# Eight of the 22 down-projection rows as four pairs with seven products each, beside classical columns of the other half of the tokens

## The chip, the cores and the metric

The kernel runs on one core of one Trainium2 chip. The metric is the device time of one execution in microseconds (us); the profile's span runs from its first to its last instruction. PE is TensorE, DVE VectorE, ACT ScalarE, POOL GpSimd, SP SyncE (all bulk DMAs are issued from its queue).

## The reference, cut to what matters

One layer of a hybrid decoder for 1024 prompt tokens and 64 sample tokens, 1088 columns in all, with shared weights. After input projection, sparse attention and short convolution comes the part that matters here:

```
def ffn_and_ple(x, p, norm_ffn, w_gate_up, w_down, norm_ple, w_ple, w_ple_gate):
    h = rmsnorm(x, norm_ffn)
    gu = h @ w_gate_up                       # 1024 -> 2 * 2816
    g, u = gu[..., :D_FF], gu[..., D_FF:]
    x = x + (jax.nn.silu(g) * u) @ w_down    # 2816 -> 1024
    gate = jax.nn.sigmoid(rmsnorm(x, norm_ple) @ w_ple_gate)
    return x + (p @ w_ple) * gate
```

All in float32. D_FF = 2816 is 22 blocks of 128, called rows here; D_MODEL = 1024 is 8 blocks, called k.

## The kernel before

**Precision.** Each float32 operand is split into a rounded `hi` part (ScalarE copy to fp32r) and the remainder `lo` (a subtraction on VectorE or GpSimd). A product is three matmuls: hi x hi, hi x lo, lo x hi.

**Layout.** The 1088 tokens lie along the free dimension and are cut into two problems p = 0 and 1 of PW = 544 columns, each of two tiles of CW = 272. The residual stream x1 lies in SBUF for the whole second half. Gate-up results go to DRAM (`m_scr`, one row of 544 columns at a time) and come back for the down projection.

**Gate-up** already uses seven products. `add_pair` loads four weight blocks and forms four sums on VectorE (`wsum`); `prep` copies each of seven combinations to `hi` on ScalarE, and `low` subtracts, on VectorE for kinds 6, 5 and 4, on GpSimd for the others. `factors` builds the seven token combinations of a problem (`fac[p]`, 28 tiles of 272 in a buffer `A` for problem 0, `B` for problem 1). `run_pair` runs 7 x 12 = 84 matmuls a pass; `GateUp.take` adds each product out of PSUM on VectorE (product 1 on ScalarE). The entries of `order` run one pair for problem 0 and then for problem 1; only the pairs 0 and 1 run for problem 0 alone, then pair 2 for both, then 0 and 1 for problem 1.

**Down projection before** (`down_pass`, `run_rows`, `down_rows`, `evac_down`). The 22 rows are four groups, `GR = [(0, 4), (4, 6), (10, 6), (16, 6)]`, which take the buffers A and B in turn. `down_rows` fetches the rows of a group for both problems into small places (`Q`, ten of 544 columns) and `row_in` splits them, every other one on GpSimd. `run_rows` makes, for one k, one PSUM tile per column tile out of all rows of the group; `evac_down` adds it to x1 on VectorE. Groups 0 and 3 use tiles of 272 columns, groups 1 and 2 three tiles of 384, 384 and 320. Groups 0 to 2 run both problems k by k; group 3 runs problem 0 for all k and then problem 1, so that problem 0's norm (`add_square`, `rstd`, `norm_rows`, which writes h3 into A) lies beside problem 1's matmuls. Then the gate pass (`ple_pass`) of each problem follows on h3.

**Order.** All instructions are put in a fixed order by `Weaver`, a planner with a cost for each operation: streams are generators, a main stream issues the matmuls, side streams are taken first when their event, places and planned times allow it. Weights are prepared ahead in eight slots and up to four raw places (`Weights.pump`), five PSUM banks `pj` take the products. The planner's costs know nothing of engines that hinder each other. TensorE's order is written out in `order`.

Of the kernel before, what the change touches and what calls it, by code (L numbers as in the profile page):

```python
# [20 lines left out]
P = 128  # L21
# [295 lines left out]
def hybrid_decoder_step(ctx, tc, I, O):  # L317
# [87 lines left out]
    class Weights:  # L405
# [114 lines left out]
        def prep(self, it, s):  # L520
# [42 lines left out]
            def low():  # L563
                (W.tt if kind in (6, 5, 4) else W.pool_tt)(flat(l), src, flat(h).bitcast(F32), OP.subtract, n)
                it["split"] = True
                self.free(*free)
# [1401 lines left out]
    def norm_rows(p, gfun, ev):  # L1968
# [4 lines left out]
        yield ev_left  # L1973
        if p == 0:
            N_["h3"] = [Rows(apool, f"A_{e}", f"h3_{e}") for e in ("hi", "lo")]
# [101 lines left out]

    ev_ms = [[Ev(), Ev()] for _ in range(NF)]
    GR = [(0, 4), (4, 6), (10, 6), (16, 6)]
# [5 lines left out]
    def down_rows():  # L2085

        for g, (f0, n) in enumerate(GR):
            free = ev_gu[g] if g < 2 else ev_gr[g - 2]
            yield ev_near
            for p in range(2):  # L2090
                left, ahead = [n], []
                for j in range(n):
                    yield ev_ms[f0 + j][p]
                    yield {"Q": 1}
                    q, = getq(1)
                    ahead.append((j, q, W.dma(q, m_scr[f0 + j, :, p * PW:(p + 1) * PW])))
                    if free.t is None and len(ahead) < min(4, n):
                        continue
                    if g not in M:
                        yield free  # L2100
                        r = "AB"[g % 2]
                        M[g] = [Rows(apool if r == "A" else N_["bp"], f"{r}_{e}", f"m{g}_{e}", n) for e in ("hi", "lo")]
                    for j_, q_, t in ahead:
                        W.spawn(row_in(M[g], j_, p, q_, t, left, ev_md[g][p]))
                    ahead.clear()

    def row_in(rows, j, p, q, t, left, ev):
        W.cur.t = max(W.cur.t, t)
        yield None
        s = split_row(rows, j, p, q, j % 2 == 1)  # L2110
        next(s)
        yield None
        next(s, None)
        left[0] -= 1
        if left[0] == 0:
            ev.t = W.cur.t

    def evac_down(g, k, p, h, ps):
        c0, n = DOWN_H[p][h] if p in DOWN_H else (p * PW + h * CW, CW)
        xs = N_["x1"][:, k, c0:c0 + n]  # L2120
        W.tt(xs, ps[:, :n], xs, OP.add, n)
        free_ps()
        if g == len(GR) - 1 and h == 1:
            W.spawn(add_square(p, k, n_down, g_ple, ev_h3, how=norm_rows))

    DOWN_H = {f"c{c}": {c // 2: CH[c]} for c in range(3)}
# [182 lines left out]
    def down_pass(g, ks, ps):  # L2309
        f0, n = GR[g]  # L2310
        bs = [rows_of(I["w_down"], k, lambda *a: evac_down(g, *a), row0=f0 * P, nk=n) for k in ks]
        evs, halves = ev_md[g], None
        if 0 < g < len(GR) - 1:
            ps, halves, evs = tuple(DOWN_H), DOWN_H, dict(zip(DOWN_H, (evs[0], evs[1], evs[1])))
        order.append(("rows", bs, ps, lambda: M[g], evs, 0, ev_gr[g] if ks[-1] == KT - 1 else None, None, halves))
# [13 lines left out]
    for g_ in range(len(GR) - 1):  # L2329
        down_pass(g_, (0, 1), (0, 1))  # L2330
        for k_ in range(2, KT):
            down_pass(g_, (k_,), (0, 1))
    n_before = len(order)
    for p_ in range(2):
        for k_ in range(KT):
            down_pass(len(GR) - 1, (k_,), (p_,))
# [35 lines left out]
    def run_pair(x, p, last, ev_done):  # L2372
        items, sink = x
        yield ev_h2[p]
        blocks = range(4)
        tot = 3 * len(blocks)
        for q_, i in enumerate(ORDER):
# [8 lines left out]
            for kk, b in enumerate(blocks):  # L2386
                th, tl = factor(p, i, b)
# [117 lines left out]
```

## Time and profile before

| | |
|---|---|
| median of 3 runs | 1964.89 us |
| profiled execution | 1964.83 us |
| its span | 1963.1 us |
| TensorE busy | 1911.7 us, 97% |
| VectorE, ScalarE, GpSimd busy | 65%, 36%, 38% |
| granted TensorE clock, mean | 0.992 |
| gate-up: matmuls from 1098.3 to | 1571.4 us |
| down projection | 1571.8 to 1837.0 us |
| gate pass and final norm | 1837.0 to 1963.1 us |

A window's line gives its length and each engine's busy time with its count of instructions in parentheses, in the order PE, PEld (weight loads), DVE, ACT, POOL, then the granted clock, DMA share and GB/s. A timeline line gives start, duration, engine, line, operation, out<-in and count, with idle time before it and its releaser in brackets.

### The profile page before, as it was taken

The page shows a single profiled execution, that of the slowest core. Times are in us where ns is not written, and L with a number is a line of the kernel's source. Part 1 is how long each engine was busy: PE and PEld are TensorE (multiplying, and loading weights), DVE is VectorE, ACT ScalarE, POOL GpSimd, SP SyncE. Part 2 cuts the span into 40 slices and gives each one's busy share as a digit, 9 for nine tenths or more (in the row PEclk, how much of TensorE's full clock was granted, in tenths as well). Part 3 has the DMA queues.
Part 4 walks back from the last instruction along what each step waited for, and adds up shares of the span by engine and source line. Part 5 has one row for each costly group of instructions (what it writes and reads, how often), then busy time and mean ns, then how long its engine had stood idle before and what let it go on. Part 6 is the DMA issues. An engine that isn't in the chain of part 4 may idle for free.

```text
span 1963.1 us, 35813 instructions
## 1 busy us (share of the span) xinstructions
PE 1911.7 (97%) x13337; PEld 1852.5 (94%) x13337; DVE 1278.8 (65%) x2691; ACT 701.7 (36%) x1403; POOL 750.5 (38%) x662
## 2 busy tenths in 40 slices
PE   8999989999999999999999899999999999999998
PEld 5998889998999989989999899999999999999998
DVE  6646999999999975214338885665665643314754
ACT  5355433213443235323334542322322322213543
POOL 2543455223322233114444342322322454424883
PEclk9999999999999999999999999999999999999999
DMA  4565335222322222546443432222222443212343
GB/s 154 170 190 151 99 105 145 54 56 66 85 65 52 63 74 54 154 126 198 126 146 121 145 101 76 77 83 70 79 83 66 139 150 99 89 47 85 105 135 118
DMA packets 293688, 206.27 MB, mean 105 GB/s; under 512 B 28912, under 2 KB 273192, under 8 KB 293514
## 3 DMA queue, kind: packets, MB, share of 16 engines
q1 hardware_dynamic: 293190, 203.63, 35.1%
q8 instruction: 105, 1.72, 0.4%
q14 instruction: 69, 0.57, 0.1%
q10 hardware_dynamic: 324, 0.36, 0.1%
HBM read 152.61 MB, written 51.31 MB: 104 GB/s over the span
## 4 chain that ended last, share of the span: by engine, by line
PE 81%; DVE 9%; issue 3%; DMA 3%; POOL 2%; SPq 1%; ACT 0%; DVEq 0%; POOLq 0%; ACTq 0%
PE pj L155 44%; PE pj L191 26%; PE at L187 4%; PE po L187 3%; PE pt L198 3%; DVE junk L1235 2%; SPq L164 1%; DVE ru L136 1%; POOL wl L151 1%; DVE cum L1271 1%; PE at L198 1%; DMA wraw<-in_w_in 1%; DMA qh<-qh_scr 0%; DVE scores L140 0%; DVE cv L140 0%
## 5 line engine op out<-in xcount | busy, mean ns | idle before, releaser
L151 POOL TENSOR_TENSOR wl<-wraw,wh 128x512 fp32r<-128x512 f32 (+2 forms) x234 | 302.4, 1295 | 660.2 <-ACT wh L132 636.5
L191 PE MATMUL pj<-h_hi,wh 128*128 128x384 f32 (+2 forms) x1197 | 404.9, 338 | 0.6 <-DVE ru L136 0.3
L191 PE MATMUL pj<-h_hi,wl 128*128 128x384 f32 (+2 forms) x1197 | 394.0, 329 | 0.7 <-POOL wl L151 0.7
L191 PE MATMUL pj<-h_lo,wh 128*128 128x384 f32 (+2 forms) x1197 | 393.6, 329 | 0.0
L132 ACT ACTIVATE wh<-wraw 128x512 fp32r<-128x512 f32 (+2 forms) x234 | 142.3, 611 | 295.8 <-PE pj L155 136.7
L191 PEld LDWEIGHTS pj<-h_hi,wh 128*128 128x128 f32 (+1 forms) x1197 | 226.4, 189 | 10.7 <-issue 6.3
L191 PEld LDWEIGHTS pj<-h_lo,wh 128*128 128x128 f32 (+1 forms) x1197 | 226.3, 189 | 2.8
L191 PEld LDWEIGHTS pj<-h_hi,wl 128*128 128x128 f32 (+1 forms) x1197 | 225.7, 189 | 1.8 <-POOL wl L151 1.1
L155 PE MATMUL pj<-f_hi,wl 128*128 128x272 f32 x704 | 204.3, 290 | 5.5 <-DVE wl L136 5.5
L155 PE MATMUL pj<-f_hi,whl 128*128 128x272 f32 x1056 | 206.0, 288 | 0.0
L155 PE MATMUL pj<-f_hi,wh 128*128 128x272 f32 x704 | 204.0, 290 | 0.3 <-DVE q_lo L136 0.2
L155 PE MATMUL pj<-f_lo,wh 128*128 128x272 f32 x704 | 203.3, 289 | 0.2 <-DVE f_lo L136 0.2
L136 DVE TENSOR_TENSOR x<-pj,x 128x272 f32<-128x272 f32 (+2 forms) x144 | 67.0, 469 | 173.4 <-PE pj L155 170.0
L155 PE MATMUL pj<-m_hi,wh 128*128 128x272 f32 (+2 forms) x586 | 176.1, 300 | 1.2 <-DVE x L136 0.7
L155 PE MATMUL pj<-m_hi,wl 128*128 128x272 f32 (+2 forms) x586 | 175.7, 300 | 0.0
L155 PE MATMUL pj<-m_lo,wh 128*128 128x272 f32 (+2 forms) x586 | 175.5, 300 | 0.0
L155 PEld LDWEIGHTS pj<-f_hi,whl 128*128 128x128 f32 x1056 | 168.7, 189 | 0.0
L155 PE MATMUL pj<-f_lo,whl 128*128 128x272 f32 x528 | 152.3, 288 | 0.0
L155 PEld LDWEIGHTS pj<-f_hi,wl 128*128 128x128 f32 x704 | 133.6, 190 | 5.9 <-DVE wl L136 5.9
L155 PEld LDWEIGHTS pj<-f_hi,wh 128*128 128x128 f32 x704 | 133.4, 189 | 0.6 <-issue 0.6
L155 PEld LDWEIGHTS pj<-f_lo,wh 128*128 128x128 f32 x704 | 133.3, 189 | 0.4 <-DVE f_lo L136 0.4
L151 POOL TENSOR_TENSOR whl<-wraw,whl 128x512 fp32r<-128x512 f32 x68 | 94.2, 1388 | 74.0 <-ACT whl L132 72.0
(376 smaller groups left out, 4488.1 us busy)
## 6 DMA issues: line engine op xcount, KB each, us to landing
wraw<-in_w_in SPq DMA_DIRECT2D x112, 256.0 KB
wraw<-in_w_gate_up SPq DMA_DIRECT2D x96, 256.0 KB
wraw<-in_w_down SPq DMA_DIRECT2D x40, 256.0 KB
wraw<-in_w_out SPq DMA_DIRECT2D x32, 256.0 KB
wraw<-in_w_ple_gate SPq DMA_DIRECT2D x32, 256.0 KB
x<-in_x_prompt SPq DMA_DIRECT2D x13, 512.0 KB
m_scr<-q_lo SPq DMA_DIRECT2D x19, 272.0 KB
q_lo<-m_scr SPq DMA_DIRECT2D x18, 272.0 KB
```

The source lines that it names most:

```text
L132: self.nc.scalar.activation(out, in_, func, **kw)
L136: self.nc.vector.tensor_tensor(out, a, b, op=op)
L151: self.nc.gpsimd.tensor_tensor(out, a, b, op=op)
L155: self.nc.tensor.matmul(ps, l, r, start=start, stop=stop)
L164: self.nc.sync.dma_start(out, in_)
L187: self.nc.tensor.matmul(ps, l, r, start=start, stop=stop)
L191: self.nc.tensor.matmul(ps, l, r, start=start, stop=stop)
L198: self.nc.tensor.transpose(ps, in_, ident)
L1235: nc.vector.tensor_scalar(junk[:m, :L], score[q], cand[:m, i:i + 1].bitcast(F32), None, op0=op, op1=OP.add, accum_out=cnt[:m, i:i + 1])
L1271: nc.vector.tensor_tensor_scan(cum, eq, eq, 0.0 if last is None else last, op0=OP.add, op1=OP.bypass)
```

## The change

- `GR` becomes two groups of seven classical rows, 0 to 6 and 15 to 21. Rows 7 to 14 become four pairs of blocks (7+b, 11+b); with the output columns k and k+4 (k = 0 to 3) they form four `DownPair` items a problem, each seven products, run by `run_pair` with `down=True`.
- `pairs_for` fetches the eight rows of a problem and `factors` builds the combinations, for problem 0 in buffer B (after gate-up has left it), for problem 1 in buffer A (after group 0 has left it). Group 1's rows go into B after problem 0's last pair (`ev_sx`).
- The order in each half g is: classical rows of group g for problem 0, all eight k; then, for i = 0 to 3, the pair i of problem g and the classical column k = i of problem 1; then k = 4 to 7 of problem 1. Down weights are therefore loaded and split once for each problem. All column tiles have 272 columns.
- A pair's seven remainders are all subtracted by VectorE (`"dve"`), and all row splits too (`row_in`). `DownPair.finish` adds the two results to x1 with 544 columns each.
- The square of k for the norm waits for pair k's addition (`last_add`); `norm_rows` also waits for the last pair of problem 1 (`ev_sy`), since h3 takes buffer A.

```diff
@@ -561,7 +561,7 @@
             W.act(flat(h), src, AF.Copy, n)
 
             def low():
-                (W.tt if kind in (6, 5, 4) else W.pool_tt)(flat(l), src, flat(h).bitcast(F32), OP.subtract, n)
+                (W.tt if kind in (6, 5, 4) or kind and "dve" in q else W.pool_tt)(flat(l), src, flat(h).bitcast(F32), OP.subtract, n)
                 it["split"] = True
                 self.free(*free)
             if kind == 0:
@@ -1971,6 +1971,7 @@
         ns, ev_r = rs.pop(p)
         yield ev_r
         yield ev_left
+        yield ev_sy
         if p == 0:
             N_["h3"] = [Rows(apool, f"A_{e}", f"h3_{e}") for e in ("hi", "lo")]
         yield {"at": 2, "Q": 1}
@@ -2075,8 +2076,26 @@
                 ev_ms[f][p].t = W.cur.t + 2.5
             W.later(store)
 
+    def last_add(p, k):
+        yield ev_sk[p][k]
+        yield from add_square(p, k, n_down, g_ple, ev_h3, how=norm_rows)
+
+    class DownPair(GateUp):
+
+
+        def finish(self, p, q1, q2):
+            for q, k in ((q1, self.f), (q2, self.f + 4)):
+                yield None
+                xs = N_["x1"][:, k, p * PW:(p + 1) * PW]
+                W.tt(xs, xs, q, OP.add, PW)
+                giveq(q)
+                ev_sk[p][k].t = W.cur.t
+
     ev_ms = [[Ev(), Ev()] for _ in range(NF)]
-    GR = [(0, 4), (4, 6), (10, 6), (16, 6)]
+    GR = [(0, 7), (15, 7)]
+    F_S = 7
+    ev_fd, ev_sx, ev_sy = [Ev(), Ev()], Ev(), Ev()
+    ev_sk = [[Ev() for _ in range(KT)] for _ in range(2)]
     ev_near = Ev()
     ev_gu, ev_gr = [Ev(), Ev()], [Ev() for _ in GR]
     ev_md = [[Ev(), Ev()] for _ in GR]
@@ -2084,30 +2103,58 @@
 
     def down_rows():
 
-        for g, (f0, n) in enumerate(GR):
-            free = ev_gu[g] if g < 2 else ev_gr[g - 2]
-            yield ev_near
-            for p in range(2):
-                left, ahead = [n], []
-                for j in range(n):
-                    yield ev_ms[f0 + j][p]
-                    yield {"Q": 1}
-                    q, = getq(1)
-                    ahead.append((j, q, W.dma(q, m_scr[f0 + j, :, p * PW:(p + 1) * PW])))
-                    if free.t is None and len(ahead) < min(4, n):
-                        continue
-                    if g not in M:
-                        yield free
-                        r = "AB"[g % 2]
-                        M[g] = [Rows(apool if r == "A" else N_["bp"], f"{r}_{e}", f"m{g}_{e}", n) for e in ("hi", "lo")]
-                    for j_, q_, t in ahead:
-                        W.spawn(row_in(M[g], j_, p, q_, t, left, ev_md[g][p]))
-                    ahead.clear()
+        yield ev_near
+        yield from rows_for(0, "A", ev_gu[0])
+        yield from pairs_for(0, "B", ev_gu[1])
+        yield from rows_for(1, "B", ev_sx)
+        yield from pairs_for(1, "A", ev_gr[0])
+
+    def pairs_for(p, r, free):
+        yield free
+        pool = N_["bp"] if r == "B" else apool
+        fac["d", p] = [pool.tile([P, 28, CW], F32, tag=f"{r}_{e}", name=f"fd{p}_{e}") for e in ("hi", "lo")]
+        left = [4]
+
+        def done():
+            left[0] -= 1
+            if left[0] == 0:
+                ev_fd[p].t = W.cur.t
+        for b in range(4):
+            for f in (F_S + b, F_S + 4 + b):
+                yield ev_ms[f][p]
+            yield {"Q": 3}
+            qs, t = getq(3), 0.0
+            for q, f in zip(qs, (F_S + b, F_S + 4 + b)):
+                t = W.dma(q, m_scr[f, :, p * PW:(p + 1) * PW])
+            W.spawn(pair_in(p, b, qs, t, done))
+
+    def pair_in(p, b, qs, t, done):
+        W.cur.t = max(W.cur.t, t)
+        yield None
+        yield from factors(("d", p), b, *qs, Ev(), done)
+
+    def rows_for(g, r, free):
+        f0, n = GR[g]
+        for p in range(2):
+            left, ahead = [n], []
+            for j in range(n):
+                yield ev_ms[f0 + j][p]
+                yield {"Q": 1}
+                q, = getq(1)
+                ahead.append((j, q, W.dma(q, m_scr[f0 + j, :, p * PW:(p + 1) * PW])))
+                if free.t is None and len(ahead) < min(4, n):
+                    continue
+                if g not in M:
+                    yield free
+                    M[g] = [Rows(apool if r == "A" else N_["bp"], f"{r}_{e}", f"m{g}_{e}", n) for e in ("hi", "lo")]
+                for j_, q_, t in ahead:
+                    W.spawn(row_in(M[g], j_, p, q_, t, left, ev_md[g][p]))
+                ahead.clear()
 
     def row_in(rows, j, p, q, t, left, ev):
         W.cur.t = max(W.cur.t, t)
         yield None
-        s = split_row(rows, j, p, q, j % 2 == 1)
+        s = split_row(rows, j, p, q, False)
         next(s)
         yield None
         next(s, None)
@@ -2116,14 +2163,13 @@
             ev.t = W.cur.t
 
     def evac_down(g, k, p, h, ps):
-        c0, n = DOWN_H[p][h] if p in DOWN_H else (p * PW + h * CW, CW)
+        c0, n = p * PW + h * CW, CW
         xs = N_["x1"][:, k, c0:c0 + n]
         W.tt(xs, ps[:, :n], xs, OP.add, n)
         free_ps()
         if g == len(GR) - 1 and h == 1:
-            W.spawn(add_square(p, k, n_down, g_ple, ev_h3, how=norm_rows))
-
-    DOWN_H = {f"c{c}": {c // 2: CH[c]} for c in range(3)}
+            W.spawn(last_add(p, k))
+
     PLE_H = {0: {0: (0, CW), 1: (CW, CW)}, 1: {"a": SEG["a"], "b": SEG["b"]}}
     pw = {}
 
@@ -2306,13 +2352,18 @@
             for p in ps:
                 order.append(("pair", x, p, p == ps[-1], ev_gu[p] if f == NF - 1 else None))
 
-    def down_pass(g, ks, ps):
+    def down_pass(g, ks, ps, ev_done=None):
         f0, n = GR[g]
-        bs = [rows_of(I["w_down"], k, lambda *a: evac_down(g, *a), row0=f0 * P, nk=n) for k in ks]
-        evs, halves = ev_md[g], None
-        if 0 < g < len(GR) - 1:
-            ps, halves, evs = tuple(DOWN_H), DOWN_H, dict(zip(DOWN_H, (evs[0], evs[1], evs[1])))
-        order.append(("rows", bs, ps, lambda: M[g], evs, 0, ev_gr[g] if ks[-1] == KT - 1 else None, None, halves))
+        for k in ks:
+            bs = [rows_of(I["w_down"], k, lambda *a: evac_down(g, *a), row0=f0 * P, nk=n)]
+            order.append(("rows", bs, ps, lambda: M[g], ev_md[g], 0, ev_done if k == ks[-1] else None))
+
+    def down_pairs(ks, ps, ev_done=None):
+        for k in ks:
+            x = pair_of(I["w_down"], F_S * P, 4, k * P, (k + 4) * P), DownPair(k)
+            x[0][0]["pair"]["dve"] = True
+            for p in ps:
+                order.append(("pair", x, p, p == ps[-1], ev_done, True))
 
     def ple_pass(p):
         for ks in [(k,) for k in range(KT)] if p == 0 else [(0,), (1,), (2,), (3,), (4,), (5, 6, 7)]:
@@ -2326,14 +2377,14 @@
     for fs_, ps_ in (((0, 1), (0,)), ((2,), (0, 1)), ((0, 1), (1,)), (range(3, NF), (0, 1))):
         gu_pass(fs_, ps_)
     n_near = len(order) - 2
-    for g_ in range(len(GR) - 1):
-        down_pass(g_, (0, 1), (0, 1))
-        for k_ in range(2, KT):
-            down_pass(g_, (k_,), (0, 1))
-    n_before = len(order)
-    for p_ in range(2):
-        for k_ in range(KT):
-            down_pass(len(GR) - 1, (k_,), (p_,))
+    for g_ in range(2):
+        down_pass(g_, range(KT), (0,))
+        for i_ in range(4):
+            if (g_, i_) == (1, 3):
+                n_before = len(order)
+            down_pairs((i_,), (g_,), (ev_sx, ev_sy)[g_] if i_ == 3 else None)
+            down_pass(g_, (i_,), (1,))
+        down_pass(g_, range(4, KT), (1,), ev_gr[0] if g_ == 0 else None)
     for p_ in range(2):
         ple_pass(p_)
 
@@ -2369,9 +2420,9 @@
                     wts.pump()
                     yield None
 
-    def run_pair(x, p, last, ev_done):
+    def run_pair(x, p, last, ev_done, down=False):
         items, sink = x
-        yield ev_h2[p]
+        yield (ev_fd if down else ev_h2)[p]
         blocks = range(4)
         tot = 3 * len(blocks)
         for q_, i in enumerate(ORDER):
@@ -2384,7 +2435,7 @@
             ps, c = psum("pj"), 0
             wts.want(it)
             for kk, b in enumerate(blocks):
-                th, tl = factor(p, i, b)
+                th, tl = factor(("d", p) if down else p, i, b)
                 for w_, a_ in ((it["hi"], th), (it["hi"], tl), (it["lo"], th)):
                     W.mmg(ps[:, :CW], w_[:, kk, :], a_, CW, c == 0, c == tot - 1)
                     c += 1
```

## Rows read from the trace of the kernel before

**Rows 1.** the page, busy time of the engines and shares of the chain.

```profile
PE 1911.7 (97%) x13337; PEld 1852.5 (94%) x13337; DVE 1278.8 (65%) x2691; ACT 701.7 (36%) x1403; POOL 750.5 (38%) x662
...
PE 81%; DVE 9%; issue 3%; DMA 3%; POOL 2%; SPq 1%; ACT 0%; DVEq 0%; POOLq 0%; ACTq 0%
```

**Rows 2.** windows of the down projection: groups 0, 1 and 3.

```profile
1571.80:1620.20 48.40, 47.75 (x381) 47.56 (x380) 20.79 (x39) 12.80 (x23) 24.59 (x19) 1.00 0.49 149
1620.20:1691.90 71.70, 71.70 (x438) 71.70 (x437) 21.67 (x31) 15.38 (x29) 27.00 (x22) 1.00 0.32 100
...
1763.50:1837.00 73.50, 73.50 (x585) 73.31 (x584) 42.78 (x80) 30.12 (x55) 43.51 (x37) 1.00 0.30 89
```

**Rows 3.** TensorE's waits after 1000 us: total, times, longest.

```profile
PE pj L155 <- DVE wl L136: 5.5, 2, 4.3
```

**Rows 4.** VectorE's timeline: evacuations of groups 0, 1 and 3.

```profile
1590.35 0.44 DVE L136 TENSOR_TENSOR x<-pj,x 128x272 f32<-128x272 f32 x1 [0.48 <-PE pj L155]
...
1620.52 0.44 DVE L136 TENSOR_TENSOR x<-pj,x 128x272 f32<-128x272 f32 x1 [1.04 <-PE pj L155]
...
1638.31 0.49 DVE L136 TENSOR_TENSOR x<-pj,x 128x320 f32<-128x320 f32 x1 [2.15 <-PE pj L155]
...
1691.71 0.49 DVE L136 TENSOR_TENSOR x<-pj,x 128x320 f32<-128x320 f32 x1 [2.08 <-PE pj L155]
...
1769.68 0.44 DVE L136 TENSOR_TENSOR x<-pj,x 128x272 f32<-128x272 f32 x1 [1.82 <-PE pj L155]
...
1799.15 0.44 DVE L136 TENSOR_TENSOR x<-pj,x 128x272 f32<-128x272 f32 x1 [1.57 <-PE pj L155]
```

**Rows 5.** ScalarE's timeline in gate-up: product 1, three pairs apart.

```profile
1351.33 0.40 ACT L132 ACTIVATE q<-pj 128x272 f32<-128x272 f32 x1 [0.38 <-PE pj L155]
...
1414.63 0.40 ACT L132 ACTIVATE q_hi<-pj 128x272 f32<-128x272 f32 x1 [0.38 <-PE pj L155]
```

**Rows 6.** VectorE's timeline in gate-up: operations back to back.

```profile
1114.58 0.68 DVE L136 TENSOR_TENSOR wsum<-wraw,wsum 128x512 f32<-128x512 f32 x1
1115.18 0.68 DVE L136 TENSOR_TENSOR whl<-wraw,whl 128x512 fp32r<-128x512 f32 x1
...
1121.82 0.43 DVE L136 TENSOR_TENSOR q_hi<-pj,q_hi 128x272 f32<-128x272 f32 x1
1122.17 0.42 DVE L136 TENSOR_TENSOR q_lo<-pj,q_lo 128x272 f32<-128x272 f32 x1
...
1134.60 0.72 DVE L136 TENSOR_TENSOR f_lo<-q,f_hi 128x544 fp32r<-128x544 f32 x1
1135.23 0.72 DVE L136 TENSOR_TENSOR f_lo<-q_hi,f_hi 128x544 fp32r<-128x544 f32 x1
```

**Rows 7.** lines by form, VectorE and GpSimd, down projection: busy us, mean ns.

```profile
L136 DVE TENSOR_TENSOR m_lo<-q_lo,m_hi 128x544 fp32r<-128x544 f32 x5 | 7.9, 1579 | 0.7 <-ACT m_hi L132 0.7
...
L151 POOL TENSOR_TENSOR wl<-wraw,wh 128x512 fp32r<-128x512 f32 x24 | 31.8, 1328 | 12.3 <-ACT wh L132 12.2
...
L151 POOL TENSOR_TENSOR wl<-wraw,wh 128x256 fp32r<-128x256 f32 x18 | 13.8, 764 | 63.9 <-ACT wh L132 63.9
```

**Rows 8.** windows of gate-up: its first pairs and its end.

```profile
1120.00:1130.00 10.00, 5.57 (x36) 5.16 (x36) 9.93 (x17) 3.46 (x7) 3.47 (x3) 0.90 0.26 82
...
1140.00:1167.00 27.00, 27.00 (x216) 27.00 (x216) 23.31 (x36) 10.88 (x20) 14.08 (x9) 1.00 0.35 110
...
1560.50:1571.80 11.30, 11.30 (x92) 11.30 (x91) 9.70 (x13) 7.41 (x14) 9.70 (x7) 1.00 0.61 185
```

**Rows 9.** TensorE's timeline: the longest wait for VectorE.

```profile
1127.78 0.40 PE L155 MATMUL pj<-f_hi,wl 128*128 128x272 f32 x1 [4.34 <-DVE wl L136]
```

**Rows 10.** timelines of VectorE and GpSimd: the norm of problem 0.

```profile
1806.10 0.21 DVE L1910 TENSOR_SCALAR ns<-po 128x4 f32<-128x4 f32 x2 [2.01 <-PE po L187]
...
1811.46 1.03 DVE L145 TENSOR_SCALAR q<-ident,ns 128x128 f32<-128x128 f32 x5
...
1826.16 1.35 POOL L151 TENSOR_TENSOR h_lox<-q_lo,h_hix 128x544 fp32r<-128x544 f32 x1
```


## Prediction

> **What bounds the kernel now.** I read the page's busy shares first. TensorE is busy 97% of the span, and the chain that ended last lies on it for 81% of its length [rows 1]. So I count matmuls first and look for waits second. The windows by stage come next [rows 2]. The down projection runs from 1571.8 to 1837.0 us, 265.2 us, and in it TensorE is idle once, 0.65 us in the first window. The reader should also see VectorE there: 20.8 of 48.4 us in group 0, 21.7 of 71.7 in group 1 (group 2 repeats it), then 42.8 of 73.5 in group 3. It has slack, and the change spends that slack. Last, the table of waits shows the one place after 1000 us where TensorE waited for VectorE: 5.5 us, in the first gate-up pairs [rows 3].
>
> **TensorE, before.** Every column tile takes rows x 3 matmuls into one bank, and VectorE's evacuation marks its end, so distances between evacuations give the price. Group 0 (4 rows, 272 columns): 20 tiles in 30.17 us, 1.509 each, 0.1257 us a matmul. Groups 1 and 2 (6 rows, tiles of 384, 384 and 320): six k in 53.40 us, 8.90 us a k. Group 3 (6 rows, 272): 13 tiles in 29.47 us, 2.267 each [rows 4]. The stage has 32 x 1.509 + 16 x 8.90 + 32 x 2.267 = 48.3 + 142.4 + 72.5 = 263.2 us. With the 0.65 us of idle time that is 263.9 of the 265.2 measured, and the rest is the norm's small products.
>
> **TensorE, after.** Seven rows are 21 matmuls a tile, 21 x 0.1258 = 2.642 us, and there are 2 groups x 8 k x 4 tiles = 64 of them: 169.1 us. A pair pass is 84 matmuls. ScalarE takes product 1 of each problem's pass, and three pairs for both problems last 63.30 us [rows 5], so one pass is 10.55 us. Eight passes are 84.4 us. The sum is 253.5 us, 9.7 us less. Roughly 12 us come from 96 matmuls fewer, and some 2.7 us are lost because four tiles of 272 (9.07 us a k of six rows) replace 384, 384 and 320 (8.90). The profiled execution took 1964.83 us (span 1963.1 and 1.7 around it), 0.06 us under the median, so without any new wait the kernel would take 1955.1 us. All the rest is whether VectorE keeps up.
>
> **VectorE's prices.** Back to back with GpSimd quiet, starts are 0.63 us apart at 544 elements, 0.60 at 512 and 0.35 at 272 [rows 6]. Beside GpSimd subtractions the 544 form takes 1.58 us instead of 0.72, an excess of 0.86 us [rows 7]. I charge 0.86 us for each GpSimd subtraction that falls among VectorE operations with two SBUF inputs; the floor is nothing, the ceiling the whole GpSimd operation, 1.33 us at 512 and by interpolation to the 0.76 of 256 some 1.05 at 384 [rows 7].
>
> **A pair with its classical column.** New on VectorE per pair: four sums and seven remainders, 11 x 0.60 = 6.6; seven additions out of PSUM, 2.45; two 544 additions into x, 1.26; the two evacuations of the classical k beside it, 0.7. That is 11.0 us. GpSimd has only the two remainders of the classical weights, 1.7 us of excess, and for problem 1 a square's addition is 0.6: 12.7 to 13.3 us. TensorE needs 10.55 + 2 x 2.642 = 15.8 us. So it fits with 2.5 to 3 us over. The nearest row is the stretch of gate-up in which pairs 0 and 1 run for one problem: TensorE is busy all 27.0 us with VectorE at 23.3 and ScalarE at 10.9 [rows 8]. There a pair has only 10.55 us, so I take no loss here. The bounds are nothing and, with each GpSimd remainder at its ceiling, 0.7 us more a step, which the 2.5 us still cover.
>
> **The two stretches ahead of the pairs.** The factors of a problem's eight rows (seven per block: four operations of 272, three remainders of 544, one of 272) cost 4 x (5 x 0.35 + 3 x 0.63) = 14.6 us. They lie beside the 16 tiles of problem 0's classical rows, 42.3 us. In the first such stretch VectorE also has seven row splits of problem 1 (4.4), evacuations (5.6), the first pair's weights (6.6) and 16 GpSimd remainders (13.8): 45.0 us, 2.7 over. In the second, problem 1's rows were split earlier, in the 26 us after the last pair of problem 0. In their place stand seven square additions (4.4) and the small operations of the norm (an estimate, 2.5: a dozen instructions at about the 0.21 us of the first, [rows 10]): 47.5 us, 5.2 over. The floor is no wait, as the order is planned with factors early, weights are prepared some eight items ahead of use, and seven products follow one another 1.5 us apart. The ceiling is the whole excess. I take half, nearer to neither end: 4 us of waits. A wait here also has an aftermath: TensorE waited 4.34 us until 1127.78 [rows 9], and in that 10 us window the granted clock reads 0.90, with VectorE busy 9.93 us [rows 8]. I add 0.5 us.
>
> **Entry.** Group 0 had four rows split by VectorE and GpSimd in turn; now seven rows of problem 0, all by VectorE, are wanted within the last gate-up pass. VectorE was already busy 9.70 of 11.3 us there with eight splits shared [rows 8]. Seven alone cost 4.4 against four contended ones; the last three of them are fetched only after the buffer is free. Between nothing and 2.5 us: I take 0.5, as a wait of 0.65 us stands there already.
>
> **Exit.** The norm of problem 0 now waits for the last pair of problem 1, because h3 takes the buffer of its factors. Queued behind that wait is everything of h3: 16 scaled products, eight copies, eight subtractions, and first gate matmuls on TensorE. Behind the last pair stand ten tiles, 26.4 us. The same chain took from 1811.46 to 1827.5 us, 16.1 us [rows 10]. Ten us are left, so nothing; at worst, with ten GpSimd remainders more in its way, 8.6 us of this cover are used up.
>
> **Loads.** Down weights go from 28 to 44 row blocks per k, 14.7 to 23.1 MB, all on SyncE's queue together with the rows that come back from DRAM; a weight load that waits for VectorE's remainder holds a row's load behind it. A pair with its column asks 1.51 MB in 15.8 us, 95 GB/s. In the 27 us without a wait 110 GB/s were moved [rows 8], so this is hidden. The row splits that leave GpSimd give nothing back by themselves: no matmul of the stage waited for GpSimd.
>
> **Sum.** 1964.83 - 9.7 + 4 + 0.5 + 0.5 = 1960.1; I predict 1960.
>
> **Rivals.** *VectorE becomes the bound of the two stretches (slower).* If each GpSimd remainder keeps VectorE out for its whole length, 16 of them cost 8 x (1.33 + 1.05) = 19.0 us instead of 13.8, and the stretches need 50.2 and 52.7 us against 42.3: 18.3 us of waits, with 1 us of clock 1955.1 + 19.3 = 1974.4. It decides from 9.7 us of waits on. For it: VectorE at 99% where the 5.5 us of waits stand, at the entry of gate-up, also beside factors [rows 3, 8]. Against it: that entry had 10.55 us a pair, and the measured excess was 0.86.
>
> The Trainium skill ("SBUF — State Buffer", Who interferes with whom) says that a VectorE instruction with two SBUF inputs and a GpSimd instruction that reads SBUF exclude each other, the second blocking fully. The trace agrees on the direction (1.58 against 0.72 us) but not on the size of it, and by the rule the time would be this rival's 1974.
>
> *No wait at all.* The eight items of lead swallow the excess: 1955, or 1954.5 if the 0.65 us go too. For it: the planner's order and no wait in the gate-up's single passes. *The hand-overs cost.* Seven rows at entry late by 2.5 us, h3 by up to 5: 1960 + 7 = 1967. *The change saves no matmul time:* if products on mixed tiles ran slower than 10.55 us a pass, 0.01 us a matmul on 672 would eat 6.7 us, 1967; nothing in the even 21.10 us steps speaks for it.
>
> **How the numbers follow.** Forecast, 1956 to 1964: 0.52. VectorE-bound, 1965 to 1980: 0.28. No wait, 1954 to 1956: 0.12. Hand-overs or slower products: 0.08. The range 1954 to 1976 holds the forecast, the no-wait case and most of the rest, and leaves out the far end of the VectorE case and mishaps. A measurement of this kernel can tell about 2% from no change, 39 us. The TensorE sum cannot give 39 us, so faster gets 0.01. Slower by 39 us needs 49 us of waits, more than twice the worst count: 0.03. Within: 0.96.
>
> **What would show it.** The stage's matmuls should go from 1824 (960 of 272 columns and 864 wider) to 2016, all of 272; the stage from the first down matmul to h3's first should last 256 to 261 us. Waits of TensorE on VectorE should stand at the first product of each problem's pairs, some us in all, with VectorE near full in the stretch before. Pair steps should be 15.8 us apart. I am wrong if waits stand inside the pair steps, at the first h3 matmul, or if VectorE's operations beside GpSimd's are longer than 1.6 us.

## The result and the profile after

The changed kernel took 1953.36 us (median of 6 runs, 1952.97 to 1958.48) against 1964.72 of the kernel before: a ratio of 0.995, 95% interval 0.994 to 0.996. That is 11.4 us less, where 4.7 were forecast, and 0.6 us under the lower end of the range; by the prediction's own mark of 2% it counts as within. One of the six executions of the kernel before took 3744 us, an outlier; the other five lie between 1962.8 and 1967.67. A second set of five runs (e11 below) gave 1956.58 against 1964.26, 7.7 us less, 0.9956 (0.9942 to 0.997).

The page's busy line shows TensorE 11.3 us shorter than in [rows 1] and VectorE at 70% instead of 65%:

```profile
span 1951.8 us, 36560 instructions
## 1 busy us (share of the span) xinstructions
PE 1900.4 (97%) x13529; PEld 1842.0 (94%) x13529; DVE 1374.3 (70%) x2873; ACT 740.3 (38%) x1475; POOL 718.1 (37%) x632
```

The windows of the down stage answer to [rows 2]. They are the rows ahead of problem 0's pairs, its pair steps, the rows behind, then the same for problem 1 (columns as there: length, PE, PEld, DVE, ACT, POOL, clock, DMA share, GB/s):

```profile
1569.80:1615.00 45.20, 42.56 (x334) 41.96 (x333) 41.97 (x67) 20.20 (x38) 17.01 (x12) 1.00 0.59 180
1615.00:1678.50 63.50, 63.50 (x508) 63.50 (x508) 45.38 (x84) 24.85 (x46) 16.03 (x14) 1.00 0.40 119
1678.50:1699.60 21.10, 21.10 (x171) 21.10 (x170) 13.42 (x20) 9.53 (x18) 9.64 (x9) 1.00 0.63 201
1699.60:1742.00 42.40, 42.40 (x337) 42.40 (x336) 37.97 (x63) 20.91 (x39) 13.77 (x11) 1.00 0.38 115
1742.00:1805.50 63.50, 63.50 (x506) 63.31 (x505) 49.66 (x102) 23.18 (x43) 16.66 (x13) 1.00 0.36 106
1805.50:1828.00 22.50, 22.50 (x182) 22.50 (x181) 18.34 (x30) 12.16 (x21) 20.31 (x14) 1.00 0.25 73
```

TensorE is idle in the first stretch only, 2.6 us. VectorE fills 93% of that stretch and 90% of the second one ahead of pairs (1699.60 to 1742.00), where TensorE waits for nothing. A pair step holds 11.3 us of VectorE for problem 0 and 12.4 for problem 1 (a quarter of 45.38 and 49.66), where I had 12.7 and 13.3. TensorE's waits after 1000 us, total, times and longest, beside [rows 3]:

```profile
PE pj L155 <- DVE wl L136: 5.5, 2, 4.3
PE pj L155 <- DVE x L136: 2.6, 3, 1.3
```

The 5.5 us in gate-up are the old ones. The new 2.6 us end with an evacuation (`x`), not with a factor or a weight. TensorE's timeline places them:

```profile
1591.23 0.36 PE L155 MATMUL pj<-m_hi,wh 128*128 128x272 f32 x1 [0.57 <-DVE x L136]
1595.39 0.39 PE L155 MATMUL pj<-m_hi,wh 128*128 128x272 f32 x1 [1.30 <-DVE x L136]
1604.39 0.36 PE L155 MATMUL pj<-m_hi,whl 128*128 128x272 f32 x1 [0.76 <-DVE x L136]
```

VectorE's timeline around the second of them, and GpSimd's one operation there, show why:

```profile
1590.66 0.43 DVE L136 TENSOR_TENSOR x<-pj,x 128x272 f32<-128x272 f32 x1
1591.01 1.70 DVE L136 TENSOR_TENSOR fd_lo<-q_hi,fd_hi 128x544 fp32r<-128x544 f32 x3
1592.63 1.53 DVE L136 TENSOR_TENSOR q_lo<-q_lo 128x272 f32<-128x272 f32 x1
1594.19 0.79 DVE L136 TENSOR_TENSOR q_lo<-q_hi,q_lo 128x272 f32<-128x272 f32 x2
1594.90 0.78 DVE L136 TENSOR_TENSOR x<-pj,x 128x272 f32<-128x272 f32 x2
```

```profile
1592.57 1.29 POOL L151 TENSOR_TENSOR whl<-wraw,whl 128x512 fp32r<-128x512 f32 x1 [2.14 <-ACT whl L132]
```

Six factor operations, 3.9 us, stand between two evacuations. One of them began during GpSimd's subtraction and took 1.53 us, where this form takes 0.43 alone. TensorE makes a tile in 2.64 us, so the PSUM banks run out while full ones stand behind factors that nobody needs before 1615 us.

### The profile page after: what moved, and what is told of

Same layout as the page of the kernel before. It is cut to its first block, busy times and chain, and to the rows that moved or that the text cites. A ratio compares the mean times of both kernels' runs of the same rounds, so it can differ in the third digit from the quotient of the medians.

```text
span 1951.8 us, 36560 instructions
## 1 busy us (share of the span) xinstructions
PE 1900.4 (97%) x13529; PEld 1842.0 (94%) x13529; DVE 1374.3 (70%) x2873; ACT 740.3 (38%) x1475; POOL 718.1 (37%) x632
## 5 line engine op out<-in xcount | busy, mean ns | idle before, releaser
L151 POOL TENSOR_TENSOR wl<-wraw,wh 128x512 fp32r<-128x512 f32 (+2 forms) x230 | 307.7, 1342 | 676.6 <-ACT wh L132 625.6
L191 PEld LDWEIGHTS pj<-h_hi,wh 128*128 128x128 f32 (+1 forms) x1197 | 225.6, 188 | 10.5 <-issue 6.4
L132 ACT ACTIVATE wh<-wraw 128x512 fp32r<-128x512 f32 (+2 forms) x243 | 149.5, 618 | 225.0 <-PE pj L191 127.5
L155 PE MATMUL pj<-m_hi,wh 128*128 128x272 f32 x482 | 139.6, 290 | 2.4 <-DVE x L136 1.9
L155 PE MATMUL pj<-m_hi,wl 128*128 128x272 f32 x482 | 139.2, 289 | 0.0
L155 PE MATMUL pj<-m_lo,wh 128*128 128x272 f32 x482 | 139.1, 289 | 0.0
L1235 DVE TENSOR_SCALAR_CACHE_REDUCE junk<-scores,canda 128x384 uint8<-128x384 f32 (+3 forms) x132 | 107.3, 813 | 4.7
```

The source lines that it names most:

```text
L132: self.nc.scalar.activation(out, in_, func, **kw)
L151: self.nc.gpsimd.tensor_tensor(out, a, b, op=op)
L155: self.nc.tensor.matmul(ps, l, r, start=start, stop=stop)
L191: self.nc.tensor.matmul(ps, l, r, start=start, stop=stop)
L1235: nc.vector.tensor_scalar(junk[:m, :L], score[q], cand[:m, i:i + 1].bitcast(F32), None, op0=op, op1=OP.add, accum_out=cnt[:m, i:i + 1])
```

## The experiments

Single executions differ by some microseconds ahead of the stage that was changed, so each trace was cut into parts: the last matmul of the input projection, the down stage from the end of gate-up to the first matmul on h3, and what follows to the end of the span (from the first and last starts of the matmuls that read `h_hi` and `f_hi`). The difference of medians is against the kernel before, measured beside it; "waits" are those of the stage's products on other engines.

| run | median us | minus before | projection ends | down | tail | waits in down |
|---|---|---|---|---|---|---|
| before | 1964.89 | | 972.3 | 265.6 | 126.1 | 0.65 |
| changed | 1953.36 | -11.4 | 969.9 | 258.5 | 123.8 | 2.6 |
| e1 before again | 1963.59 | -0.9 | 973.1 | 265.5 | 125.7 | 0.5 |
| e2 eight products | 1970.03 | +5.5 | 974.5 | 270.6 | 124.4 | 2.6 |
| e3 before, tiles of 272 | 1964.94 | +0.4 | 969.5 | 268.0 | 125.4 | 1.0 |
| e4 pairs in a row | 1955.97 | -8.5 | 971.2 | 258.9 | 123.3 | 2.5 |
| e5 GpSimd remainders | 1955.94 | -7.2 | 971.1 | 259.7 | 124.4 | 3.5 |
| e6 GpSimd rows | 1955.57 | -7.5 | 970.2 | 259.1 | 124.5 | 2.2 |
| e7 seven twice | 1970.32 | +7.2 | 973.9 | 271.3 | 124.6 | 10.5 |
| e8 three twice | 1955.14 | -8.0 | 971.8 | 258.5 | 123.6 | 2.5 |
| e9 no GpSimd | 1952.67 | -11.6 | 971.1 | 255.3 | 124.8 | 0 |
| e10 factors later | 1953.24 | -11.0 | 975.5 | 255.2 | 123.7 | 0 |
| e11 changed again | 1956.58 | -7.7 | 972.8 | 258.5 | 124.6 | 2.5 |
| e12 gate-up too | 1957.13 | -7.7 | 973.4 | 255.3 | 123.3 | 0 |

The projection is the same code in all of them and ends between 969.5 and 975.5 us: this is the scatter that the medians of five or six runs still carry. The down stage repeats to 0.1 us (265.6 and 265.5, 258.5 twice).

**e1, e11: both kernels again.**

> The kernel before, once more, for a second trace of its stages. If the 4.2 us by which the two traces differ outside the down projection (1.9 us before its first matmul, 2.3 us behind the first matmul on h3) are scatter of single executions, this trace has them elsewhere: first down matmul at 1569.5 to 1572 us, gate pass of 124 to 126 us. If they belong to the change, this trace repeats 1571.8 and 126.1 us to 0.5 us. Down projection 265 us by both.

> The changed kernel once more. Its median stood 2 us below the variants that should cost nothing, whose stage times agree with it to 1 us. If that is scatter of the stretch ahead of the down projection (its end lay between 969.5 and 974.5 us in nine traces), this gives 1953 to 1956 us and a down stage of 258.5 us; if those variants cost something, it repeats 1953.4 us.

e1's down stage repeats; its gate-up ended at 1573.0 us, outside both guesses and 1.6 us after the first trace of the same kernel (1571.4), so the 1.9 us ahead of the stage are scatter. Its tail of 125.7 decides nothing by itself; with the other traces below it speaks for a real part. e11 gave 1956.58, 0.6 us above its guess, with the same down stage of 258.5: the first median was some 2 us on the lucky side, and the variants of the same stage time cost nothing that these medians show.

**e2: the seventh's gain taken away.**

```diff
-            ps, c = psum("pj"), 0
+            ps = psum("pj")
+            for rep in range(2 if down and i == 2 else 1):
+                c = 0
...   12 matmuls of the product, as before
```

> The changed kernel in which the 12 matmuls of product 2 are run twice in each of the eight down passes (the second run starts the sum anew), so TensorE runs as many matmuls as with eight products; nothing else changes. Theory (the gain is TensorE's count): 96 x 0.1256 = 12.1 us more, 1965.4 us, no quicker than the kernel before. Rival (the gain comes from the order, the splits or the tail, and TensorE has slack beside VectorE in the pair steps): less than 6 us more, below 1959.5 us.

The down stage went from 258.5 to 270.6 us: 12.1, the forecast to 0.1. The median moved by more, 16.7 us over the first median and 13.5 over e11's; the projection ended 4.6 us later in its trace. The rival is out: with eight products the kernel is slower than before (ratio 1.0029, 1.0017 to 1.0042), so the count of matmuls is the whole gain of the stage.

**e3: the narrower tiles alone.**

```diff
-        if 0 < g < len(GR) - 1:
+        if False:
             ps, halves, evs = tuple(DOWN_H), DOWN_H, dict(...)
```

> The kernel before in which groups 1 and 2 use four column tiles of 272 instead of 384, 384 and 320. Theory (a matmul costs its columns and a small fixed part, so 288 more matmuls for the same columns cost 2.7 us): 1967.4 us. Rival (the tile width costs nothing, the matmul stream is limited by columns alone): 1964.7 us.

The down stage grew by 2.5 us, 0.5 of it wait: 2.0 us for the tiles, not 2.7. The median's +0.4 us (ratio 1.0006, 0.9997 to 1.0015) cannot tell it from nothing; the stage can.

**e4: no classical columns between the pairs.**

```diff
             down_pairs((i_,), (g_,), ...)
-            down_pass(g_, (i_,), (1,))
-        down_pass(g_, range(4, KT), (1,), ev_gr[0] if g_ == 0 else None)
+        down_pass(g_, range(KT), (1,), ev_gr[0] if g_ == 0 else None)
```

> The changed kernel with the four pairs of a problem one after the other and the other problem's eight classical columns behind them: TensorE has 10.55 us a pair instead of 15.8. Theory (VectorE's demand of 10.3 to 11.6 us a pair without the classical column just about fills 10.55 us, and the lead of eight prepared items covers the rest): 0 to 5 us more, 1953 to 1958 us, with waits of TensorE on VectorE in the pair steps. Rival (the columns between are what makes the pairs fit): VectorE and the weight loads cannot keep up, over 10 us more, above 1963 us.

Nothing: 258.9 us and no wait in the pair steps. The window of four bare pairs shows VectorE at 85% with TensorE full:

```profile
1615.00:1660.00 45.00, 45.00 (x361) 45.00 (x360) 38.17 (x72) 18.10 (x34) 7.07 (x5) 1.00 0.34 98
```

The interleaving is not what makes the pairs fit here.

**e5, e6: the remainders and the row splits back on GpSimd.**

```diff
e5 -            x[0][0]["pair"]["dve"] = True
e6 -        s = split_row(rows, j, p, q, False)
e6 +        s = split_row(rows, j, p, q, j % 2 == 1)
```

> The changed kernel with GpSimd instead of VectorE subtracting the remainders of products 1, 7, 2 and 3 of the down pairs, as in gate-up; row splits stay with VectorE. Theory (VectorE has 3 us to spare in a pair step, so which engine subtracts is free there): 1953.4 us, within 1.5 us, the down stage within 1 us of 258.5. Rival (the move to VectorE is part of the gain, because GpSimd's six subtractions of some 1.4 us a step hold VectorE up): over 3 us more, waits of TensorE on GpSimd's remainders or on VectorE inside the pair steps.

> The changed kernel with every other row split given back to GpSimd, as before the change. Theory (the 2.6 us of waits between 1591 and 1604 us stand where VectorE is full from 1560 to 1600, with 14 row splits and the factors ahead of the evacuations): three of seven splits a problem leave VectorE, 3.8 us less on it, and the waits fall below 1.5 us: 1952 to 1953 us. Rival (GpSimd beside VectorE costs VectorE 0.86 us a split, more than the 0.63 saved): the waits stay or grow, 1953.5 to 1956 us.

e5 cost 1.2 us of stage, just over the 1 us that its theory allowed, 0.9 of it more wait in the same place, none inside the pair steps. e6 has two waits, at 1592.23 and 1596.65 us, both in front of products of a classical column (`m_hi`), as in the changed kernel. The profile puts the longer one down to a copy of ScalarE; VectorE's evacuation had ended 0.1 us before that copy did, and had begun 4.8 us after the evacuation ahead of it:

```profile
PE pj L155 <- ACT fd_hi L132: 1.8, 1, 1.8
PE pj L155 <- DVE x L136: 0.4, 1, 0.4
```

The stage is 0.6 us longer, and behind the longer wait the granted clock fell, which in the changed kernel it did not:

```profile
1590.00:1600.00 10.00, 7.82 (x50) 7.31 (x49) 9.90 (x18) 5.30 (x11) 3.40 (x3) 0.83 0.60 177
```

That alone is worth 1.7 us (17% of 10 us, an estimate). The waits did not fall below 1.5 us, so the theory of e6 fails; the rival's numbers came (2.2 us of waits, 1955.57 us). Its reason fits: nine splits of the stage left VectorE, 5.7 us at 0.63 each, and VectorE's operations with two SBUF inputs were held up 36.4 us beyond their bare time instead of 31.1 in the changed kernel (both counted in the traces as described under e9).

**e7, e8: how much VectorE has to spare in a pair step.** After the remainder's subtraction, for all seven products (e7) or for three (e8), the same once more, unknown to the planner:

```diff
+                if kind and "dve" in q:            # e8: kind in (1, 5, 2)
+                    nc.vector.tensor_tensor(flat(l), src, flat(h).bitcast(F32), op=OP.subtract)
```

> The changed kernel in which VectorE subtracts each of the seven remainders of a down pair twice, 4.2 us more a pair step, unknown to the planner, so the order stays. Theory (measured VectorE load of 11.8 to 12.5 us a step of 15.8, so some 3.3 us are free): 0.9 us or less over per step, mostly swallowed by the lead of eight prepared items: 0 to 7 us more, 1953.4 to 1960.5 us. Rival (VectorE's latency, not its load, sets the step, each doubled remainder on the path of its product): 8 x 4.2 = 33 us more, or at least 15.

> The same with three of the seven remainders (products 1, 5 and 2) subtracted twice, 1.8 us more a pair step. Theory (3.3 us are free in a step): no change, 1953.4 us within 1.5 us, and no wait inside the pair steps. Rival (latency on the path): 8 x 1.8 = 14 us more, or at least 5.

e8 left the down stage at 258.5 us: 1.8 us a step are free, and latency is not on the path. e7 made it 271.3, 12.8 more (13.7 in the median over e11), between the two theories and above the 7 us I had as ceiling. The loss comes late: problem 0's pairs begin at 1619.81, 1635.64, 1651.43 and 1668.15 us, so its first two steps keep their 15.8 us and the third loses 0.9; problem 1's first step loses nothing, its second and third 1.8 and 2.8. So the lead of prepared items swallows the first steps, and then each one pays. How much fits without the lead can be read from ScalarE's copies of product 1 in problem 0, which are 18.20 us apart three times: 2.3 of the 4.2 us are paid there, some 1.9 fit, which agrees with e8. The loss is not waits alone: TensorE waited some 8 us more in the pair steps, and the granted clock fell as well (0.97 in the second window). VectorE's share in the two stretches of pair steps is then 93% of both, and the waits lie at its evacuations and remainders (L566 is the added line):

```profile
1620.00:1680.00 60.00, 57.57 (x454) 56.99 (x454) 55.54 (x96) 18.47 (x35) 10.80 (x7) 1.00 0.29 84
1755.00:1815.00 60.00, 54.42 (x412) 53.17 (x411) 55.65 (x105) 19.63 (x39) 10.49 (x7) 0.97 0.28 83
```

```profile
PE pj L155 <- DVE x L136: 9.0, 10, 1.9
PE pj L155 <- DVE wl L136: 5.5, 2, 4.3
PE pj L155 <- DVE wl L566: 1.5, 2, 0.8
```

**e9, e10: two cures for the 2.6 us.** e9 lets VectorE subtract the remainders of the classical down weights too; e10 lets the planner put factors only 0.5 us ahead.

```diff
e9  -  (W.tt if kind in (6, 5, 4) or kind and "dve" in q else W.pool_tt)(...)
e9  +  (W.tt if kind in (6, 5, 4) or kind and "dve" in q or it.get("dve") else W.pool_tt)(...)
e9  +            for it, _, _ in bs[0]["units"][0]:      # in down_pass
e9  +                it["dve"] = True
e10 -        W.cur.lag = 5.0 if p == 0 else 2.5
e10 +        W.cur.lag = 0.5 if isinstance(p, tuple) else 5.0 if p == 0 else 2.5
```

> The changed kernel in which VectorE also subtracts the remainders of the classical down weights, so GpSimd does nothing between its last gate-up weights and h3. Theory (a GpSimd subtraction costs VectorE about 0.86 us beside two-input operations, more than the 0.5 to 0.6 us of doing it there): VectorE's load in the down stage does not grow, no 544 subtraction takes over 1 us there, the waits stay at 1 to 4 us, 1951 to 1955 us. Rival (the excess is small and VectorE is the scarce engine): 32 k columns x 2 remainders add 35 us to VectorE, the waits grow by over 4 us, above 1957 us.

> The changed kernel in which the planner lets the factors of the down rows go on only while VectorE is planned at most 0.5 us ahead of TensorE (2.5 before), so evacuations stand earlier in VectorE's queue. Theory (the 2.6 us of waits come from evacuations queued behind runs of factor operations): waits below 1 us, stage 256 to 257.5 us, 1.5 to 2.5 us less than the changed kernel in the same call. Rival (VectorE is simply full from 1560 to 1600 us, the order does not matter): waits of 2 us or more, as evacuation or at the first product of a pair.

Both take every wait of the products out of the down stage: 255.3 and 255.2 us, 3.9 and 3.3 us less than e11 in the medians measured together (1952.67 and 1953.24 against 1956.58). With no wait left, 255.2 is TensorE's own time: the 253.5 of the sum and 1.7 for the norm's small products. The windows from the end of gate-up to the first product of a pair hold the same work of TensorE, in the changed kernel, in e9 and in e10:

```profile
1569.40:1615.07 45.67, 43.03 (x337) 42.43 (x336) 42.44 (x68) 20.60 (x38) 17.01 (x12) 1.00 0.59 181
1570.10:1612.45 42.35, 42.35 (x338) 42.35 (x337) 38.31 (x78) 20.39 (x37) 0.00 (x0) 1.00 0.61 187
1575.30:1617.65 42.35, 42.35 (x337) 42.35 (x336) 40.20 (x68) 20.39 (x38) 16.40 (x12) 1.00 0.66 201
```

In e10 VectorE and GpSimd have the same operations there as in the changed kernel, in another order, and TensorE does not wait. That is the order, but not only the place of the evacuations: in the new order GpSimd also held VectorE up less, 2.2 us by the windows, and the two were not separated. In e9 VectorE does the subtractions of the classical weights in that stretch itself and is still busy 4.1 us less. Over the whole stage it is the other way, against the theory of e9 that VectorE's load does not grow; the changed kernel first, then e9:

```profile
1569.40:1828.00 258.60, 255.97 (x2031) 255.17 (x2030) 207.14 (x362) 111.22 (x203) 93.41 (x71) 1.00 0.43 129
1570.10:1825.40 255.30, 255.30 (x2032) 255.11 (x2031) 211.71 (x419) 111.02 (x201) 15.17 (x11) 1.00 0.43 128
```

With 60 GpSimd operations fewer, VectorE's operations with two SBUF inputs exceed their bare times (0.72 us for 544 elements, 0.68 for 512, 0.58 for 384, 0.43 for 272, with no GpSimd operation beside them) by 5.7 us in sum instead of 31.1: 0.4 us for each of the 60, less than the 0.58 or 0.68 us that VectorE takes for one. What decides the price is whether the two meet. Of the changed kernel's 71 GpSimd operations in the stage, 40 had a VectorE operation with two SBUF inputs begin during them, and 39 of these ended 0.58 us (544 elements), 0.55 (512) or 0.30 (272) after a GpSimd operation ended, so they had stood still until then; the fortieth began as GpSimd was ending. An operation out of PSUM is not held up: 30 evacuations that lie within GpSimd operations took 0.42 to 0.44 us. In the stretch ahead of problem 0's pairs all 12 of GpSimd's operations met one (10.3 us, 0.86 each), in the pair steps 9 of 27 (5.5 us). There GpSimd mostly runs beside evacuations, as in the first pair step:

```profile
1618.05 2.26 POOL L151 TENSOR_TENSOR wl<-wraw,wh 128x512 fp32r<-128x512 f32 x2 [16.07 <-ACT wh L132]
```

```profile
1618.37 0.44 DVE L136 TENSOR_TENSOR q_lo<-pj,q_lo 128x272 f32<-128x272 f32 x1 [0.54 <-PE pj L155]
1619.81 0.44 DVE L136 TENSOR_TENSOR q<-pj,q_lo 128x272 f32<-128x272 f32 x1 [1.00 <-PE pj L155]
```

The `fd_lo` subtractions of 544 elements show the price in their mean, the changed kernel first and then e9 (busy us, mean ns):

```profile
L136 DVE TENSOR_TENSOR fd_lo<-q_lo,fd_hi 128x544 fp32r<-128x544 f32 x11 | 10.1, 932 | 0.0
```

```profile
L136 DVE TENSOR_TENSOR fd_lo<-q_lo,fd_hi 128x544 fp32r<-128x544 f32 x11 | 7.8, 720 | 0.0
```

**e12: the same cure for gate-up's 5.5 us.**

```diff
-  (W.tt if kind in (6, 5, 4) or kind and "dve" in q or it.get("dve") else W.pool_tt)(...)
+  (W.tt if kind or it.get("dve") else W.pool_tt)(...)
```

> The run without GpSimd in the down stage, and VectorE also subtracts the four remainders of each gate-up pair that GpSimd had. If a GpSimd subtraction costs VectorE more (0.86 us) than doing it (0.60), the 5.5 us of waits in the first gate-up pairs, where VectorE is at 99%, shrink by 2 us or more and the gate-up stage falls from 473 to 468 to 471 us: 1948 to 1951 us. Rival (VectorE is the scarce engine there and the excess is paid only in part): the waits grow, gate-up 474 us or more, above 1953.5 us.

A miss, and the rival's numbers: gate-up took 476.9 us instead of e9's 472.9, and the waits grew. VectorE's operations are at their bare length there (the 512 subtractions at 0.68 us), but the waits went to the factors, and the clock was low for longer than in e9, whose 20 us from 1120 us on read 0.91:

```profile
PE pj L155 <- DVE f_lo L136: 4.0, 2, 2.9
PE pj L155 <- ACT f_hi L132: 2.2, 1, 2.2
...
PE pj L155 <- DVE wl L136: 0.7, 1, 0.7
PE pj L155 <- DVE whl L136: 0.6, 1, 0.6
```

```profile
1130.00:1140.00 10.00, 5.38 (x40) 4.83 (x38) 9.83 (x23) 2.26 (x5) 0.00 (x0) 0.89 0.16 54
1140.00:1150.00 10.00, 8.39 (x42) 8.09 (x43) 6.57 (x13) 3.43 (x7) 0.00 (x0) 0.59 0.08 29
```

With 7.5 us of waits instead of 5.5, the excess alone does not bound that place; what does was not separated, since the planner's order changed with it.

## Why the prediction was right, and where it was off

**TensorE's sum was right.** 253.5 us with 84 matmuls a pass and 2.642 us a tile; e9 and e10 show a stage without waits at 255.2 to 255.3, and e2 shows 96 matmuls at 12.1 us to 0.1. The stage holds the 2016 matmuls forecast and lasts 258.5 us, within the 256 to 261. The pair steps are 15.86 us apart (ScalarE's copy of product 1 at 1617.01, 1632.87, 1648.79 and 1664.58), where 15.8 was forecast; in problem 1 they are 16.1 apart on average, since the norm's small products stand in its first step. The price of the narrower tiles inside the sum was 2.0 us instead of 2.7.

**The waits were mis-sized and misplaced.** I took 4 us ahead of the pairs, 0.5 of clock and 0.5 at the entry, 5 in all; they came to 2.6 less the old 0.65, so +2.0. The step that failed is the "16 GpSimd remainders (13.8)" in each of the two stretches. The charge of 0.86 us held where the two engines met, but only 12 and 10 subtractions ran in the stretches (27 ran in the pair steps), and 12 and 9 met a VectorE operation with two SBUF inputs: 10.3 and 7.4 us in place of 13.8 each. VectorE was busy 42.0 and 38.0 us there, not the 45.0 and 47.5 of the sum, and TensorE needs 42.3: full in the first stretch, no excess. (The rest of the difference in the second stretch is work that ran elsewhere.) The waits that did come have another mechanism, which the prediction named only as a symptom ("VectorE near full in the stretch before"): evacuations stand behind factors, some of them held up by GpSimd, in VectorE's queue while it is full, and the banks run out. None stood at a first product, where I had placed them. e10 shows that the order decides it: same operations, other order, no wait.

**No rival came true.** The case without waits (1955) came nearest in number, but 2.6 us of waits were there. VectorE as the bound (1974) rested on a whole GpSimd operation lost each time. By the rule of the Trainium skill ("SBUF — State Buffer", Who interferes with whom) the second of the two blocks fully. The trace agrees, more than the prediction allowed: 39 of 40 meetings in the stage ended only after GpSimd's operation had. The time of 1974 does not follow from it, because VectorE lost the rest of GpSimd's operation, some 0.8 us a meeting of the 1.0 to 1.9 us that it lasts, and 31 of the 71 operations met nothing that they could hold up. e7 shows that this rival's mechanism is real some 1.9 us a step further on. One of my signs of being wrong did come: eleven VectorE operations of the stage lasted over 1.6 us beside GpSimd, up to 1.96. The sign was badly set, as 1.58 in [rows 7] is a mean, and the kernel before has single ones of up to 1.89.

**The hand-overs cost nothing.** No wait stood at the entry. At the exit the norm's chain ran from 1801.41 to 1818.9 us, 17.5 us, and ended 9 us ahead of the first matmul on h3 at 1828.0. It began 0.4 us after the last matmul of problem 1's pairs had ended at 1801.0, which fits the new wait having set its start, and the ten tiles behind the pairs covered it.

```profile
1801.41 2.11 DVE L145 TENSOR_SCALAR q_lo<-ident,ns 128x128 f32<-128x128 f32 x5
```

```profile
1817.54 1.38 POOL L151 TENSOR_TENSOR h_lox<-q,h_hix 128x544 fp32r<-128x544 f32 x1
```

**The tail gave more, which I had not in the sum.** It lasts 125.4 to 126.1 us in three traces with the order before and 123.3 to 124.8 in eleven with the order after, some 1.6 us less on average. Of this, 0.7 us is the norm of problem 1, whose scales came 0.9 us late for TensorE before and 0.2 us after. Another part is the clock behind that norm: one 10 us window of the gate pass, 60 us behind the first matmul on h3, reads 0.83 in all three traces of the old order and in six of the eleven of the new one, and 1.00 in the other five. The first window is of e1, the second of the changed kernel, the third of e11, which is the same kernel again:

```profile
1898.50:1908.50 10.00, 9.57 (x69) 9.46 (x68) 4.66 (x16) 4.81 (x10) 5.21 (x7) 0.83 0.43 127
```

```profile
1888.00:1898.00 10.00, 9.68 (x79) 9.42 (x79) 6.97 (x17) 5.20 (x12) 7.18 (x9) 1.00 0.39 118
```

```profile
1890.10:1900.10 10.00, 10.00 (x71) 9.97 (x71) 6.00 (x17) 4.41 (x11) 6.41 (x8) 0.83 0.37 107
```

With 0.83 the new order's tails last 124.4 to 124.8 us, with 1.00 123.3 to 123.8. So about 1 us goes with the clock, which differs between executions of one kernel and is no merit of the change; among traces with 0.83 the new order saves 1.2 us.

**The whole.** The stage gives 7.1 us and the tail 1.2 to 1.6, together some 8.5. The two measurements, 11.4 and 7.7, lie on both sides of it, by the scatter of the projection and of the clock. That the first lies under my range and the second, 1956.58, inside the 1956 to 1964 of the forecast is this scatter too, and no merit. Of the 6.7 us between my 1960.1 and 1953.4, 2.4 are the stage, where I had the waits too long (7.1 instead of 4.7), 2.3 the tails of the two first traces, and the rest scatter ahead of the stage.

## What to carry to other kernels

Where TensorE is full, saved matmuls are saved time as long as the engine that prepares them stays below full in each stretch by itself; the way to know the margin is to double a cost there (three doubled remainders a pair free, seven 12.8 us). A helper engine's price is paid where the two meet, so count the meetings in each stretch and not the operations. In front of a nearly full engine look at what stands behind what in its queue: work that is needed late, put early, makes work late that is needed soon, and moving it took the waits away (3.3 us here). Cut traces into stages before comparing runs: the stage repeated to 0.1 us where medians differed by 3.

## What the runs showed of the hardware that was not expected

A VectorE operation with two SBUF inputs that began during a GpSimd subtraction stood still until that ended: 39 of 40 ended 0.30 to 0.58 us after a GpSimd operation, while 30 evacuations out of PSUM within GpSimd operations kept their 0.42 to 0.44 us. What this costs depends on the meetings: 0.86 us a subtraction where all of them met one, 0.4 us on average over the stage, beside the 0.58 (384 elements) to 0.68 us (512) of the same subtraction on VectorE.

The granted TensorE clock has two levels in these traces, 1.00 (2.4 GHz) and half of it (1.2 GHz). It fell to the lower one after waits of 1.8 to 4.3 us (0.59 to 0.90 as the mean of 10 us windows), though not after e5's of 1.9 us, and also after pauses of at most 0.93 us each (0.83), at the same place of the pass in one execution of a kernel and not in another.
